# Hybrid attention/RG-LRU block: W loads of the first half of the tokens issued by PoolE instead of SyncE

## The chip, the cores and the metric

The kernel runs on one core of one Trainium2 chip. Five engines work beside each other, each through its own list of instructions in order: TensorE (PE in the profile; its weight loads are PEld), VectorE (DVE), ScalarE (ACT), PoolE or GpSimd (POOL) and SyncE (SP), which computes nothing here and issues most DMAs. An instruction waits for semaphores, and everything behind it on the same engine waits with it. The metric is the device time of one execution in microseconds (us), the median of several runs.

## The reference

One decoder block over 2048 tokens of width 1024. A combined projection gives q, k and v of three groups of heads, a gate of the attention, input and gate of a recurrent branch (RG-LRU), and two merge gates. Dilated banded attention and the recurrence follow; both are gated, projected, merged, projected again and normalized. The change concerns the first line of it:

```python
proj = x @ w_in[l] + b_in[l]          # (2048 x 1024) @ (1024 x 9216)
q, k, v, g_attn, u_lru, g_lru, gate_logits = jnp.split(proj, SPLIT_POINTS, axis=-1)
...
u = causal_depthwise_conv(u_lru, conv_w[l], conv_b[l])
h = rg_lru(u, lru_wr[l], lru_br[l], lru_wi[l], lru_bi[l], lru_lambda[l])
y_b = (h * jax.nn.silu(g_lru)) @ w_lru_proj[l]
```

All values are float32. The kernel splits each operand of a product into a high and a low part and forms three products of them.

## The kernel before

**Quads.** The projection takes the larger part of the time (about 0 to 1440 us of the span). It is cut into 72 quads: 36 for the first half of the tokens (`plan[s][0]` is 0, s from 0 to 35), the same 36 for the second (`plan[s][0]` is 1). A quad is two blocks of 128 output columns by two chunks of 512 tokens. Except for the first quad of all (s is 0), a quad is computed by Strassen's scheme with seven products instead of eight; their factors are blocks of W (A11, A12, A22) and sums of blocks (S1 to S4) on one side, and prepared blocks of x on the other. A product is 12 matmuls of 128x128 by 128x512 on PE (L632), four slices of depth with high and low parts. One product is one step of the program's clock `now["n"]`, and `base[s]` is the step at which quad s begins. A quad of the middle kind takes 7 steps.

**Where a block of W comes from.** `load_w` (L232) takes a slot of SBUF (one of 34, 128x512 float32, 256 KB, handed out in the order in which they became vacant) and loads a block from HBM. In the first half S1 and S3 are both loaded as A21, and then `added` (L242) adds A22 to the one and A11 to the other by an accumulating DMA, issued by POOL, that waits until the first load has landed. DVE adds S2 = S1 + A11 in `sums` and S4 = S2 + A12 in `add_w`. Then `prep_w` (L264) forms the high part on ACT (L269) and the low part on DVE (L227, a helper's line for all two-input operations). The low parts go to DRAM (L282), and the second half of the tokens loads them from there.

**The order.** It is written out ahead: events are put at steps, and each step emits its product and then its events, so each engine's list follows the steps. For the first half, with t0 four steps ahead of `base[s]`:

```python
for d, n in ((6, "S1"), (6, "S3"), (4, "A11"), (3, "A12"), (d22, "A22")):
    at(t0 - d, lambda s=s, n=n: load_w(s, n))
for n, x in (("S1", "A22"), ("S3", "A11")):
    at(max(t0 - 4, 2), lambda s=s, n=n, x=x: added(s, n, x))
...
at(max(t0 - 1, 4), lambda s=s: sums(s))
at(max(t0, 4), lambda s=s: add_w(s, "S4", "S2", "A12"))
```

For a quad of the middle kind `d22` is -1, so its A22 falls into the step of the S1 and S3 of the next quad, ahead of them.

**What else is in these lists.** SP issues, beside the loads of W: the swaps of halves for the rotary embedding (L307, four DMAs of 64 KB for each block of q or k), the stores of k, q, v (L330, L337, L347, L371), of gates and of the recurrence's input (L377, L396, L411, L419), and the low parts (L282). POOL has, in the first half, the accumulating DMAs, the loads of the small gate matrices (`fetch_gr`, L441, four of 16 KB each) and the product of the recurrence's result with its gate (L540, shown as L227 y<-y,h), which waits for the scan on DVE (L528). The gate matmuls of the recurrence (L493, output g) stand on PE between two halves of a product and read vh (ACT, L483) and vl (DVE).

After the projection come attention (to about 1650 us), the merge, and the output projection with the normalization; the change touches nothing there.

Of the kernel before, what the change touches and what calls it, by code (L numbers as in the profile page):

```python
# [15 lines left out]
P = 128  # L16
S = 2048
# [14 lines left out]
def hybrid_block_kernel(ctx: ExitStack, tc: tile.TileContext, a: dict, out: bass.AP):  # L32
    nc = tc.nc
    sp, act, dve, pool, pe = nc.sync, nc.scalar, nc.vector, nc.gpsimd, nc.tensor
# [98 lines left out]
    def take(name, dt=F32R):  # L133
        if not vacant:
            raise RuntimeError(f"no slot at {now['n']}: {[x[1].name if hasattr(x[1],'name') else x[1] for x in home.values()]} chains {len(chains)}")
        i = vacant[0]
        if name[0] == "y" and now["n"] >= base[NQ - 1]:
            i = next((x for x in LATE if x in vacant), i)
            if i in LATE:
                LATE.remove(i)  # L140
        vacant.remove(i)
        t = sl_p.tile([P, CH], dt, tag=f"s{i}", name=name)
        home[id(t)] = (i, t)
        return t
# [86 lines left out]

    def load_w(s, n):  # L232
        r = raw[s, n] = take(f"w{n}_{s}", F32)
        sp.dma_start(r.rearrange("p (k f) -> p k f", f=P), w_part(s, "A21" if n[0] == "S" else n))

    def w_part(s, n):

        f = plan[s][1][int(n[1]) - 1][0]
        k = 4 * (int(n[2]) - 1)
        return a["w_in"][f, :, k:k + 4, :]  # L240
# [318 lines left out]
    plan = []  # L559
# [142 lines left out]
    for s in range(1, NQ):  # L702
        t0 = base[s] - (3 if plan[s][0] else 4)
        if plan[s][2] is None:
            for d, n in ((4, "A21"), (4, "A11"), (3, "A22"), (3, "A12")):
                at(t0 - d, lambda s=s, n=n: load_w(s, n))
            for j in range(4):
                at(t0 + j, lambda s=s, j=j: prep_w(s, j))
            continue
        if plan[s][0]:  # L710
            for d, n in ((4, "A21"), (4, "A22"), (3, "A11"), (3, "A12")):
                at(t0 - d, lambda s=s, n=n: load_w(s, n))
        else:
            d22 = 3 if s == 1 else 4 - plan[s][2].index(4)
# [6 lines that stand above are left out]
        if plan[s][0]:  # L721
            at(t0, lambda s=s: sum3(s))
        for j in range(7):
            d = 3 if j == 6 and plan[s][2] is MID else 0
            if plan[s][0] and j % 2 == 0:
                at(t0 + j - 1 + d, lambda s=s, j=j: load_lo(s, j))
            at(t0 + j + d, lambda s=s, j=j: prep_w(s, j))
# [244 lines left out]
    n = len(where)  # L972
# [416 lines left out]
    for n in range(32):  # L1389
        c, f = divmod(n, 8)  # L1390
# [229 lines left out]
```

## Time and profile before

| | us |
|---|---|
| median of 3 runs | 2099.08 |
| lowest, highest | 2097.64, 2104.75 |
| the profiled execution, its own time | 2101.99 |
| its span, first to last instruction | 2100.3 |
| DVE busy in the span | 1676.0 |
| ACT busy in the span | 1093.1 |
| loads of W by SP, both halves | 253 (wA) and 70 (wS), 256 KB each |
| accumulating loads by POOL | 70, 256 KB each |

The profile is of one execution. In its rows a line such as L234 is the line of the kernel, the names behind the operation are out<-in with numbers left out (wA is a block A11, A12, A21 or A22, wS an S1 or S3), and what stands in brackets is the idle time of the engine just before and who ended it. In lists of waits the columns are the total in us, how many, and the longest. SPq is SP's queue. A DMA's time to landing runs from its issue to the last of its data.

### The profile page before, as it was taken

To read this page: it belongs to the slowest core of one execution; us is meant where nothing else is said; L and a number is where in the kernel's file an instruction comes from. 1 tells how busy PE (TensorE), PEld (TensorE's weight loads), DVE (VectorE), ACT (ScalarE), POOL (GpSimd) and SP (SyncE) were. 2 spreads that over 40 slices of the span, in tenths; PEclk is the share of its full clock that TensorE was granted. 3 is DMA by queue.
4 is the path that set the end of the run, shared out by engine and by line. 5 is a ranking of instruction groups with operands and counts; after the bars stand their busy time and mean duration, and the time that the engine had idled before them with its cause. 6 is when DMAs were issued, how large, how long until landed. Compare 5 with 4: busy or idle time off the path is not lost. (4 is left out here: it accounts for less than half of the span.)

```text
span 2100.3 us, 35032 instructions
## 1 busy us (share of the span) xinstructions
PE 2070.4 (99%) x11696; PEld 1706.2 (81%) x11696; DVE 1676.0 (80%) x3146; ACT 1093.1 (52%) x2293; POOL 474.9 (23%) x436
## 2 busy tenths in 40 slices
PE   8999999999999999999999999999999999999998
PEld 7888788788778888888888887888888888888887
DVE  8889789788788778888879887976999645576667
ACT  6347356346256566657666565666999411211100
POOL 1111111111111012231222232221424344331120
PEclk9999999999999999999999999999999999999999
DMA  9898988998988977878788879789896798864431
GB/s 273 270 251 250 263 261 248 281 247 264 235 284 233 319 229 203 243 206 232 235 271 255 283 225 260 230 244 352 317 345 206 228 305 273 299 223 157 156 106 71
DMA packets 369589, 516.26 MB, mean 246 GB/s; under 512 B 173056, under 2 KB 178176, under 8 KB 366080
## 3 DMA queue, kind: packets, MB, share of 16 engines
q1 hardware_dynamic: 349232, 480.63, 71.6%
q0 software_dynamic: 12256, 19.42, 5.6%
q10 hardware_dynamic: 7920, 13.97, 1.9%
q8 instruction: 93, 1.52, 0.3%
q14 instruction: 88, 0.72, 0.1%
HBM read 312.95 MB, written 186.25 MB: 238 GB/s over the span
## 5 line engine op out<-in xcount | busy, mean ns | idle before, releaser
L632 PE MATMUL q<-xT,hS 128*128 128x512 f32 x1680 | 519.2, 390 | 0.5 <-DVE y L227 0.5
L632 PE MATMUL q<-xT,l 128*128 128x512 f32 x1120 | 436.2, 389 | 0.0
L632 PE MATMUL q<-xB,hA 128*128 128x512 f32 x1248 | 389.9, 394 | 5.8 <-ACT xB L215 5.8
L632 PEld LDWEIGHTS q<-xT,hS 128*128 128x128 f32 x1680 | 314.2, 188 | 70.8 <-issue 6.1
L632 PE MATMUL q<-xB,l 128*128 128x512 f32 x904 | 354.0, 392 | 5.8 <-DMA l<-wl_scr 3.5
L632 PEld LDWEIGHTS q<-xB,hA 128*128 128x128 f32 x1248 | 235.7, 190 | 59.3 <-ACT xB L215 5.7
L632 PEld LDWEIGHTS q<-xT,l 128*128 128x128 f32 x1120 | 210.6, 188 | 43.9
L632 PEld LDWEIGHTS q<-xB,l 128*128 128x128 f32 x904 | 170.8, 189 | 44.2 <-DMA l<-wl_scr 5.1
L269 ACT ACTIVATE hA<-wA 128x512 fp32r<-128x512 f32 x218 | 135.0, 622 | 86.8 <-DMA wA<-in_w_in_dram 54.5
L632 PE MATMUL q<-xT,hA 128*128 128x512 f32 x560 | 174.1, 392 | 0.0
L245 POOL DMA_DIRECT2D wS<-in_w_in_dram x70 | 62.0, 978 | 493.8 <-DMA wS<-in_w_in_dram 201.5
L1051 ACT ACTIVATE p<-p,sta 128x256 f32<-128x256 f32 (+1 forms) x384 | 172.7, 468 | 1.1 <-DVE sta L1043 1.1
L632 PE MATMUL q<-xB,hS 128*128 128x512 f32 x560 | 172.6, 389 | 0.0
L269 ACT ACTIVATE hS<-S 128x512 fp32r<-128x512 f32 x175 | 107.8, 623 | 88.9 <-DVE S L227 42.6
L227 POOL TENSOR_TENSOR S<-S,wA 128x512 f32<-128x512 f32 x35 | 50.1, 1431 | 415.6 <-DVE S L227 214.6
L632 PEld LDWEIGHTS q<-xT,hA 128*128 128x128 f32 x560 | 105.1, 189 | 24.0 <-issue 2.5
L632 PEld LDWEIGHTS q<-xB,hS 128*128 128x128 f32 x560 | 105.1, 188 | 22.1 <-issue 0.4
L227 DVE TENSOR_TENSOR y<-y,cos 128x512 f32<-128x512 f32 x96 | 85.0, 888 | 43.3 <-DMA sw<-y 38.3
L1043 DVE CUSTOM_DVE_ANT_0 p<-s,mask 128x256 f32<-128x256 f32 (+1 forms) x384 | 116.4, 360 | 0.2 <-PE s L1036 0.2
L1479 PE MATMUL z<-wo,mh 128*128 128x512 f32 (+1 forms) x264 | 101.0, 383 | 0.0
L1480 PE MATMUL z<-wo,ml 128*128 128x512 f32 (+1 forms) x264 | 101.0, 383 | 0.0
L1478 PE MATMUL z<-wo,mh 128*128 128x512 f32 (+1 forms) x264 | 101.0, 383 | 0.0
(204 smaller groups left out, 4163.6 us busy)
## 6 DMA issues: line engine op xcount, KB each, us to landing
wA<-in_w_in_dram SPq DMA_DIRECT2D x253, 256.0 KB, 5.0
wl_scr<-l SPq DMA_DIRECT2D x105, 512.0 KB, 5.3
l<-wl_scr SPq DMA_DIRECT2D x105, 512.0 KB, 4.6
sw<-y SPq DMA_DIRECT2D x384, 64.0 KB, 3.1
wS<-in_w_in_dram SPq DMA_DIRECT2D x70, 256.0 KB, 4.6
wS<-in_w_in_dram POOLq DMA_DIRECT2D x70, 256.0 KB, 6.5
v_scr<-vs SPq DMA_DIRECT2D x192, 64.0 KB, 3.9
B<-k_scr SPq DMA_DIRECT2D x24, 512.0 KB, 7.5
```

Of the source, the lines that this page charges most:

```text
L227: eng.tensor_tensor(out=out, in0=in0, in1=in1, op=op)
L245: pool.dma_start(t, w_part(s, x), accum_op=ALU.add)
L269: act.activation(h, r, AF.Copy)
L632: pe.matmul(bank, w[:, ks], x[:, kk, xx], start=(first and i == 0 and not onto), stop=(last and i == 11), skip_group_check=onto)
L1043: dve.tensor_tensor_reduce(out=st["p", i, j][:, h, lo:256], in0=st["s", i, j // 2][h][:, j % 2, lo:256], in1=mask[:, lo:256], scale=1.0, s ...
L1051: act.activation(p, p, AF.Exp, scale=-1.0, bias=s[:, h:h + 1], accum_out=s[:, 2 + h:3 + h])
L1478: pe.matmul(z, mh[:, k], w[:, 0, hs], start=(k == 0), stop=False)
L1479: pe.matmul(z, mh[:, k], w[:, 1, hs], start=False, stop=False)
L1480: pe.matmul(z, ml[:, k], w[:, 0, hs], start=False, stop=(k == 7))
```

## The change

The engine that issues the DMA in `load_w` is chosen by the quad. The second half of the tokens and the first quad stay on SP; the other 35 quads of the first half go to POOL, five loads each. Slots, destinations, bytes and the steps at which the loads stand in the program are the same.

```diff
     def load_w(s, n):
         r = raw[s, n] = take(f"w{n}_{s}", F32)
-        sp.dma_start(r.rearrange("p (k f) -> p k f", f=P), w_part(s, "A21" if n[0] == "S" else n))
+        eng = sp if plan[s][0] or not s else pool
+        eng.dma_start(r.rearrange("p (k f) -> p k f", f=P), w_part(s, "A21" if n[0] == "S" else n))
```

## The prediction

> **What bounds the kernel now.** I read the busy shares first, then the two halves of the projection stage, then TensorE's waits in the first one, since that is where the moved loads lie.
>
> ```profile
> span 2100.3 us, 35032 instructions
> PE 2070.4 (99%) x11696; PEld 1706.2 (81%) x11696; DVE 1676.0 (80%) x3146; ACT 1093.1 (52%) x2293; POOL 474.9 (23%) x436
> ...
> 0.00:720.00 720.00, 704.37 (x3086) 573.87 (x3087) 609.09 (x976) 375.86 (x619) 98.10 (x127) 1.00 0.89 262
> ```
>
> The last row is the first half of the tokens: window, its length, busy us of PE, PEld, DVE, ACT, POOL, then granted clock, DMA share, GB/s. PE is busy 704.37 of 720 us, so the loads can win only from 15.6 us of idle time and from what the clock lost. POOL works 98 us of 720. The DMA engines are at 0.89, and the change moves no byte off them.
>
> TensorE's waits in that stretch, and the table of 20 us windows around the worst place:
>
> ```profile
> PE q L632 <- ACT xB L215: 5.8, 1, 5.8
> PE g L493 <- DVE vl L227: 5.1, 2, 2.6
> PE q L632 <- DVE l L227: 2.2, 2, 1.2
> PE g L493 <- ACT vh L483: 2.0, 1, 2.0
> PE q L632 <- DVE y L227: 0.5, 1, 0.5
> ...
> 580.00:600.00 20.00, 18.09 (x68) 14.31 (x69) 16.23 (x27) 17.11 (x26) 1.75 (x2) 0.83 0.97 327
> 600.00:620.00 20.00, 20.00 (x90) 16.57 (x89) 15.96 (x24) 6.21 (x11) 5.17 (x7) 1.00 0.78 233
> ```
>
> 5.8 us is the start, before the second quad, which the change leaves alone. 9.8 us remain: 7.1 in the gate matmuls (L493), 2.7 in L632. In 580 to 600 us the granted clock was 0.83 of full speed: 20 x 0.17 = 3.4 us lost on top. So **13.2 us** is all that the first half can give.
>
> Who caused these waits? The timelines of PE, DVE and ACT at the two stalls:
>
> ```profile
> 578.93 0.51 PE L493 MATMUL g<-vh,gw 64*128 64x512 f32 x2 [2.00 <-ACT vh L483]
> 581.91 0.79 PE L493 MATMUL g<-vl,gw 64*128 64x512 f32 x2 [2.48 <-DVE vl L227]
> ...
> 577.72 0.69 DVE L227 TENSOR_TENSOR S<-wS,wA 128x512 f32<-128x512 f32 x1 [2.60 <-DMA wA<-in_w_in_dram]
> 579.96 0.69 DVE L227 TENSOR_TENSOR S<-S,wA 128x512 f32<-128x512 f32 x1 [0.75 <-DMA wA<-in_w_in_dram]
> ...
> 577.73 0.63 ACT L269 ACTIVATE hA<-wA 128x512 fp32r<-128x512 f32 x1 [5.13 <-DMA wA<-in_w_in_dram]
> ...
> 261.86 0.50 PE L493 MATMUL g<-vl,gw 64*128 64x512 f32 x2 [2.64 <-DVE vl L227]
> ...
> 259.91 0.69 DVE L227 TENSOR_TENSOR S<-S,wA 128x512 f32<-128x512 f32 x1 [1.93 <-DMA wA<-in_w_in_dram]
> ```
>
> Both engines stood still for a block of W that had not landed: ACT 5.13 us, DVE 2.60 and 0.75, and, 318 us earlier, DVE 1.93. vh and vl, which the gate matmuls read, are queued behind these on ACT and DVE. So 2.00 + 2.48 + 2.64 = 7.1 us of PE idle, and the clock loss that follows the first pair at once, come from W loads that were late. Why late? SP's own timeline ahead of the second stall:
>
> ```profile
> 560.44 3.08 SPq L307 DMA_DIRECT2D sw<-y  x4
> ...
> 564.75 0.91 SPq L234 DMA_DIRECT2D wS<-in_w_in_dram  x2
> ...
> 566.91 3.02 SPq L377 DMA_DIRECT2D u_scr<-y  x1
> 569.98 1.61 SPq L371 DMA_DIRECT2D v_scr<-vs  x1
> 571.64 0.67 SPq L234 DMA_DIRECT2D wA<-in_w_in_dram  x1
> ...
> 573.31 1.26 SPq L234 DMA_DIRECT2D wA<-in_w_in_dram  x1
> ```
>
> Between the S loads and the A11 load, 6.9 us pass in which SP issues stores; one of them holds it 3.02 us, another 1.61. A11 was issued at 571.64 and ended the waits at 577.7, 6.1 us later. SP's order, not the transfer, made it late.
>
> **The change part by part.** For quads 1 to 35 five loads (S1, S3, A11, A12, A22) go from SP to POOL: 175 DMAs of 256 KB, the same bytes. The accumulating DMAs (L245) stay on POOL.
>
> ```profile
> L245 POOL DMA_DIRECT2D wS<-in_w_in_dram x70: 853/909/1244, 19.3 to 686.7; - x70
> ...
> DMA to landing us min/median/max: 3.8/6.5/9.1
> ...
> L441 POOL DMA_DIRECT2D gr<-in_wr_dram x32: 526/556/1220, 64.4 to 1325.0; - x32
> ...
> DMA to landing us min/median/max: 2.0/5.3/7.4
> ...
> DMA to landing us min/median/max: 2.7/4.6/9.5
> ```
>
> (Issues of the accumulating loads and their landing; of the 16 KB gate blocks and theirs; the last row is the landing of SP's W loads in 0 to 720.)
>
> A plain 256 KB load by POOL is not in this trace. Its issue lies between 0.56 (16 KB) and 0.91 us (same size, accumulating); I take 0.91, the row of the same size. From issue to landing it lies between SP's 4.6 and the accumulating 6.5; I take 6.5, again the row of POOL's own loads of this size. So each load costs 1.9 us more than on SP, once issued.
>
> POOL's load: per quad 7 DMAs x 0.91 = 6.4 us. A quad is 84 matmuls at 90 per 20 us, 18.7 us. Over 35 quads 175 x 0.91 = 159 us more on an engine that is busy 98 of 720: it fits, at no cost beside the order.
>
> Order on POOL: A22 of the old quad, S1, S3, A11, the two accumulates, A12. A12, and all of the next quad, now stand behind the accumulates' wait for S1 and S3. Suppose POOL began exactly at the step where the program places these loads. A22 starts at 0, S1 at 0.9, S3 at 1.8; S1 lands at 0.9 + 6.5 = 7.4, its accumulate starts then and lands at 13.9. The sum that needs it comes five steps of 12 matmuls later, 5 x 12 x 0.222 = 13.3 us: 0.6 us late (with 4.6 for the plain load, 1.3 early). The second accumulate starts at 8.3, A12 at 9.2 and lands at 15.7; it is needed at six steps, 16.0. What covers the 0.6 is that POOL need not wait for its step:
>
> ```profile
> SPq L234 <- DVE l L227: 16.3, 10, 3.7
> SPq L234 <- PE q L632: 4.7, 10, 0.8
> SPq L234 <- PE g L493: 4.1, 2, 2.9
> ...
> POOL wS L245 <- DMA wS<-in_w_in_dram: 201.5, 16, 23.9
> POOL y L227 <- DVE h L528: 79.7, 11, 13.7
> ```
>
> The first three rows are SP's largest waits for engines at the W loads, 25 us in 22 of 183 loads (113 and 70): mostly the slot was already free when SP came to it, so a queue with less in front issues earlier. POOL stood idle 201.5 us in 16 waits for S blocks issued by SP: it is ahead of SP, not behind. If the cover fails, DVE waits 0.6 us per quad, which its own lead over PE hides; only several us at once reached PE above.
>
> A bound on the other side: the W stalls of 577 to 582 us began with a load issued 6.9 us after the S loads. Even with 1.9 us more per transfer, 5 us are won there.
>
> SP loses 175 issues. By its median rows a W load holds it about half a microsecond, some 90 us of 720, so its other work comes earlier, above all the half swaps that DVE waits for:
>
> ```profile
> L234 SPq DMA_DIRECT2D wA<-in_w_in_dram x113: 327/518/3436, 0.8 to 717.3; - x113
> ...
> DVE y L227 <- DMA sw<-y: 35.9, 19, 3.7
> ...
> 555.41 0.69 DVE L227 TENSOR_TENSOR y<-y,cos 128x512 f32<-128x512 f32 x1 [1.41 <-DMA sw<-y]
> ...
> 558.62 0.50 PE L632 MATMUL q<-xB,l 128*128 128x512 f32 x1 [1.20 <-DVE l L227]
> ```
>
> The remaining 2.7 us of PE idle (L632) follow such DVE waits: 3 us before the 1.20 at 558.62 DVE had waited 1.41 for swapped halves. I count half of 2.7, 1.4 us; the ends are 0 and 2.7. It costs nothing where it fails.
>
> **Sum:** 7.1 + 3.4 + 1.4 = 11.9 us. The profiled execution took 2101.99 us (span 2100.3), so 2090.1. The median of the runs shown is 2099.08, 2.9 us less; theirs reach from 2097.64 to 2104.75, and I take it that they differ by just such stalls, so I don't subtract that again.
>
> [...] The rows of L245 show POOL issuing in 0.85 to 1.24 us while DVE was busy 609 of 720 us. [...]
>
> **The rivals.**
>
> *A. Loads in time, stalls gone:* the forecast, 2088.8 (all of 13.2) to 2093.
>
> *B. Hidden anyway.* The stalls are two accidents out of 35 quads. With DMA at 0.89, POOL's loads now compete with SP's stores instead of standing behind them; stores land later, slots come free later, and another quad gets the accident. For it: the share, and that DVE is busy 609 of 720, so little else gives way. Against it: no byte is added. If the larger stall (2.00 + 2.48 + 3.4 = 7.9) comes back once, 2090.1 + 7.9 = 2098.
>
> *C. POOL's order takes SP's place (slower).* POOL waits in order too: for h (L528) 79.7 us in 11 waits, at most 13.7, and for the slot of A11, ahead of the accumulates. Lead and need differ by 0.6 us the wrong way, so from the point where POOL begins a quad some 5 us behind its step (the length of the ACT wait that reached PE), PE stands, and the clock halves. Three such quads instead of the two now: 3 x 7.9 = 23.7, minus the 11.9 won, 2101.99 + 11.8 = 2114. POOL's idle time above speaks against it.
>
> *D. It does nothing.* If slots rather than SP set the issue of the loads, they move by nothing: 2099 to 2102. The waits at slots (25 us in 183 loads) speak against it.
>
> [...]
>
> **How the numbers follow.** A 0.55, B 0.26, C 0.12, D 0.04, E 0.03. A run of this kernel can be told from no change beyond some 0.3%, 6.3 us, that is below 2092.8 or above 2105.4. Most of A is faster, some of it within; B, D and E are within; C is slower. Faster 0.53, same 0.35, slower 0.12. Predicted 2090. The range leaves out C and a little of A's edge: low 2085 (all 13.2 with the runs' 2.9 below the profile), high 2102 (D).
>
> **What would show it.** Right: the W loads of a quad issued by POOL ahead of their old times, by 5 us or more at the old stalls; no wait of L493 over 1 us and no window of clock under 1.00 in the first half; ACT's and DVE's waits for wA near zero; fewer DVE waits for sw. Wrong: POOL waits for slots or for h with an accumulate behind, S sums waiting for wS, PE waits in other quads. If POOL's issue of a plain load is far over 0.91 us, or its landing over 6.5, the sum falls.

## The result and the profile after

| | before | after |
|---|---|---|
| median of 4 runs | 2098.55 us | 2121.55 us |
| lowest, highest | 2097.64, 2104.75 | 2118.53, 2122.74 |
| ratio, 95% interval | | 1.0101 (1.0079 to 1.0124) |
| the profiled execution | 2101.99 us | 2122.74 us |

The change made the kernel slower by 1%, 23 us. The prediction said 2090 with a range of 2085 to 2102, so the time lies outside it, and the kernel became slower where it was to become faster. In the rows of after, lines from 234 on have moved by one (L632 is L633, L307 is L308, L245 is L246, L493 is L494); the load of W is L235.

The head of the page of after, two rows of the table of windows (window, length, busy us of PE, PEld, DVE, ACT, POOL, granted clock, DMA share, GB/s), and TensorE's and VectorE's waits in the first half:

```profile
span 2121.0 us, 35087 instructions
...
PE 2077.7 (98%) x11696; PEld 1707.7 (81%) x11696; DVE 1678.5 (79%) x3146; ACT 1093.1 (52%) x2293; POOL 574.1 (27%) x611
```

```profile
260.00:280.00 20.00, 14.32 (x57) 10.92 (x56) 14.23 (x23) 9.62 (x17) 3.21 (x6) 0.83 0.93 246
580.00:600.00 20.00, 14.36 (x53) 11.35 (x52) 11.11 (x18) 8.65 (x17) 3.98 (x7) 0.83 0.98 257
```

```profile
PE q L633 <- DVE y L227: 14.6, 5, 5.7
PE q L633 <- ACT xB L215: 7.7, 4, 5.7
...
PE g L494 <- ACT ti L506: 0.9, 1, 0.9
...
PE g L494 <- DVE vl L227: 0.6, 2, 0.3
PE g L494 <- ACT vh L484: 0.3, 2, 0.2
...
DVE y L227 <- DMA sw<-y: 62.1, 21, 7.1
```

The stalls that the change was expected to remove are gone: before the gate matmuls, vl and vh now cost 0.9 us, against 7.1 before. The first three rows that follow are of before: DVE's waits for wA and wS, which are in no row of after, and ACT's for wA. The last row is what is left of ACT's in after: three waits in the first 20 us and one at 743.7 us, behind the first half.

```profile
DVE S L227 <- DMA wA<-in_w_in_dram: 6.2, 4, 2.6
...
DVE S L227 <- DMA wS<-in_w_in_dram: 3.8, 4, 1.7
...
ACT hA L269 <- DMA wA<-in_w_in_dram: 12.4, 6, 5.1
...
ACT hA L270 <- DMA wA<-in_w_in_dram: 5.7, 4, 2.2
```

What came instead is larger. TensorE's products waited 14.6 us for DVE's y (0.5 before), and DVE waited 62.1 us for swapped halves (35.9 before). Two of the new stalls hold most of it, each with a window at clock 0.83:

```profile
266.48 1.19 PE L633 MATMUL q<-xT,hS 128*128 128x512 f32 x2 [5.68 <-DVE y L227]
...
592.29 1.19 PE L633 MATMUL q<-xT,hS 128*128 128x512 f32 x2 [5.64 <-DVE y L227]
...
264.44 0.69 DVE L227 TENSOR_TENSOR y<-y,cos 128x512 f32<-128x512 f32 x1 [6.81 <-DMA sw<-y]
...
590.25 0.69 DVE L227 TENSOR_TENSOR y<-y,cos 128x512 f32<-128x512 f32 x1 [6.78 <-DMA sw<-y]
```

DVE stood 6.8 us at a swap, and the result that TensorE's next matmul waits for (y<-q, at 265.65 us) is queued behind it. Each of the two costs 5.6 to 5.7 us of idle, and some clock behind it: from 264 to 270 us the granted clock was 0.50 (as in before from 582 to 588 us), in part while TensorE stood still anyway. The 20 matmuls across the two stalls took 12.2 and 13.0 us, where 20 x 0.227 = 4.5 us is their pace elsewhere, so the two cost 7.7 + 8.5 = 16.2 us together.

**Where the time is lost.** If the start of the n-th matmul of after is set against that of before, after is 7.1 us late at the 42nd matmul (18.4 us in before) and still at the 504th, 20.0 late at the 3016th (704 us) and 19.7 late near the end. So all of it is lost in the first half, and a third of it in the first 20 us. The other 12.9 us are a difference: before had lost 13.2 us to its own stalls, which are gone, so the new ones behind the start cost some 26 us by estimate, twice as much.

**The start.** The timelines of POOL and SP of after, and SP's of before:

```profile
2.06 1.31 POOL L235 DMA_DIRECT2D wS<-in_w_in_dram  x2
3.36 1.60 POOL L235 DMA_DIRECT2D wA<-in_w_in_dram  x3
9.00 1.93 POOL L246 DMA_DIRECT2D wS<-in_w_in_dram  x2 [4.04 <-DMA wS<-in_w_in_dram]
...
10.32 10.01 SPq L221 DMA_DIRECT2D xcB<-in_xT_dram  x8
```

```profile
7.59 5.62 SPq L221 DMA_DIRECT2D xcB<-in_xT_dram  x8
```

POOL's list is empty at 2 us, so it issues the five W blocks of the second quad and both accumulates while SP still brings x for the first. The eight x loads began 2.7 us later and took 10.01 us to issue instead of 5.62, so the last was out 7.1 us later, the loss of the start. In both runs SP starts each of the eight 0.02 us after an earlier load has landed, and by 26 us it had waited 8.3 us for such landings ahead of x loads, against 3.1 in before. Before, the W blocks stood behind x in SP's list, from 13.59 us on.

**The swaps.** Around 255 us, in the timeline of after: SP's four DMAs of the fourth swap of a q/k pair, and POOL.

```profile
255.24 5.15 SPq L308 DMA_DIRECT2D sw<-y  x4
...
254.06 0.54 POOL L235 DMA_DIRECT2D wA<-in_w_in_dram  x1 [5.94 <-DVE rp L227]
254.59 1.86 POOL L246 DMA_DIRECT2D wS<-in_w_in_dram  x2
...
257.09 0.57 POOL L235 DMA_DIRECT2D wA<-in_w_in_dram  x1 [0.64 <-DMA k_scr<-rp]
```

The four issues of that swap in after, in the view of its line (least/median/most ns), and the swap, the W loads behind it and the accumulates in the timelines of SP and POOL of before:

```profile
L308 SPq DMA_DIRECT2D sw<-y x4: 527/1488/1517, 255.2 to 258.9; - x4
```

```profile
240.99 3.00 SPq L307 DMA_DIRECT2D sw<-y  x4
...
244.66 0.52 SPq L234 DMA_DIRECT2D wA<-in_w_in_dram  x1
245.22 0.91 SPq L234 DMA_DIRECT2D wS<-in_w_in_dram  x2
...
249.82 1.82 POOL L245 DMA_DIRECT2D wS<-in_w_in_dram  x2 [23.93 <-DMA wS<-in_w_in_dram]
```

In after, A11, both accumulates and A12 go out between 254.06 and 257.66, and the fourth swap between 255.24 and 260.39: 1 MB of W beside 256 KB of swap. In before the accumulates were issued 8.8 us after the swap, since S1 and S3, to which they add, stood behind it on SP. A11 waited on POOL for a slot that the third block's rp gives back, 5.94 us, so its moment is tied to the q/k chain. The landing is not all of the lateness. Set against TensorE's progress (how late the same matmul starts in after), SP issued the fourth swap 3.6 us later than in before at the first of the two stalls and 0.8 at the second; from first issue to last landing it took 9.1 and 8.9 us, against 4.4 and 4.5. The landing of all swaps of the first half, before and then after (least, median, most):

```profile
DMA to landing us min/median/max: 1.9/3.0/7.6
```

```profile
DMA to landing us min/median/max: 1.9/4.1/9.9
```

### The profile page after: what moved, and what is told of

Read it like the earlier page. It is cut to its first block, busy times and chain, and to the rows that moved or that the text cites. A ratio compares the mean times of both kernels' runs of the same rounds, so it can differ in the third digit from the quotient of the medians.

```text
span 2121.0 us, 35087 instructions
## 1 busy us (share of the span) xinstructions
PE 2077.7 (98%) x11696; PEld 1707.7 (81%) x11696; DVE 1678.5 (79%) x3146; ACT 1093.1 (52%) x2293; POOL 574.1 (27%) x611
## 5 line engine op out<-in xcount | busy, mean ns | idle before, releaser
L633 PE MATMUL q<-xT,hS 128*128 128x512 f32 x1680 | 522.7, 393 | 14.6 <-DVE y L227 14.6
L633 PE MATMUL q<-xT,l 128*128 128x512 f32 x1120 | 437.2, 390 | 0.0
L633 PE MATMUL q<-xB,hA 128*128 128x512 f32 x1248 | 391.5, 395 | 8.8 <-ACT xB L215 7.7
L633 PEld LDWEIGHTS q<-xT,hS 128*128 128x128 f32 x1680 | 316.2, 189 | 86.8 <-issue 21.7
L633 PE MATMUL q<-xB,l 128*128 128x512 f32 x904 | 354.5, 392 | 6.3 <-DMA l<-wl_scr 3.4
L633 PEld LDWEIGHTS q<-xB,hA 128*128 128x128 f32 x1248 | 235.4, 189 | 65.6 <-ACT xB L215 9.6
L633 PEld LDWEIGHTS q<-xT,l 128*128 128x128 f32 x1120 | 211.3, 189 | 44.3
L633 PEld LDWEIGHTS q<-xB,l 128*128 128x128 f32 x904 | 170.9, 189 | 45.2 <-DVE l L227 5.4
L633 PE MATMUL q<-xT,hA 128*128 128x512 f32 x560 | 173.1, 390 | 0.0
L633 PE MATMUL q<-xB,hS 128*128 128x512 f32 x560 | 172.5, 389 | 0.0
L235 POOL DMA_DIRECT2D wA<-in_w_in_dram x105 | 67.5, 643 | 337.4 <-DVE l L227 123.5
L633 PEld LDWEIGHTS q<-xT,hA 128*128 128x128 f32 x560 | 104.7, 188 | 23.6 <-issue 2.2
L633 PEld LDWEIGHTS q<-xB,hS 128*128 128x128 f32 x560 | 105.0, 188 | 22.1 <-issue 0.4
```

What stands on the lines that cost most here:

```text
L235: eng.dma_start(r.rearrange("p (k f) -> p k f", f=P), w_part(s, "A21" if n[0] == "S" else n))
L633: pe.matmul(bank, w[:, ks], x[:, kk, xx], start=(first and i == 0 and not onto), stop=(last and i == 11), skip_group_check=onto)
```

## The experiments

Theory 1: POOL runs ahead of SP, and its accumulates and A loads move the same bytes at the very time of the fourth swap, which DVE needs at once; the swap lands late. Theory 2: it is the start alone, or the mere use of POOL's queue, or the A loads. All of the edits below stand in `load_w` unless another place is shown. The table gives all runs; each ratio is to the runs of before taken beside it, whose medians were 2098.55 to 2099.87 us. "Fourth swap" is the time from the first issue to the last landing of the four DMAs, least to most, in the profiled execution of each, for six of the twelve q/k pairs: those whose fourth swap landed latest in after (tiles sw12_1, sw21_1, sw22_1, sw16_1, sw23_1, sw18_1). The other six took 3.8 to 4.7 us in before and 5.0 to 7.9 in after.

| run | what goes out by POOL | median us | ratio to before, 95% interval | DVE waits for sw, us | fourth swap, us |
|---|---|---|---|---|---|
| before | accumulates | 2098.55 | | 35.9 | 3.8 to 5.8 |
| after | all loads, quads 1 to 35 | 2121.55 | 1.0101 (1.0079 to 1.0124) | 62.1 | 8.3 to 10.8 |
| e1_from_quad3 | all loads, quads 3 to 35 | 2115.00 | 1.0068 (1.0053 to 1.0083) | 66.0 | 8.1 to 10.6 |
| e2_a_on_pool | only A11, A12, A22, from quad 3 | 2099.33 | 1.0001 (0.9990 to 1.0011) | 43.8 | 5.0 to 7.1 |
| e3_s_on_pool | only S1, S3, from quad 3 | 2107.04 | 1.0033 (1.0020 to 1.0047) | 58.8 | 4.9 to 8.9 |
| e4_traffic | as before, and useless copies at the swap | 2118.08 | 1.0086 (1.0071 to 1.0101) | 61.6 | 5.3 to 8.8 |
| e5_after_swap | as e1, accumulates held behind the swap | 2099.91 | 1.0004 (0.9995 to 1.0012) | 42.1 | 3.8 to 5.2 |
| e6_start_only | all loads of quads 1 and 2 alone | 2105.89 | 1.0041 (1.0029 to 1.0054) | 40.6 | 3.8 to 6.0 |
| e7_wait_only | as before, with e5's hold | 2098.31 | 1.0001 (0.9992 to 1.0010) | 35.5 | 3.8 to 5.8 |
| e8_a_after_swap | as e2, with e5's hold | 2101.51 | 1.0014 (1.0005 to 1.0023) | 39.8 | 4.4 to 5.7 |
| e9_a12_early | as e5, A12 two steps earlier | 2097.37 | 0.9989 (0.9980 to 0.9998) | 42.4 | 4.5 to 6.4 |
| e10_a12_early_sp | as e7, A12 two steps earlier on SP | 2096.98 | 0.9990 (0.9979 to 1.0000) | 37.3 | 3.8 to 5.8 |

### The start taken out

```diff
-        eng = sp if plan[s][0] or not s else pool
+        eng = sp if plan[s][0] or s < 3 else pool
```

> As the changed kernel, but POOL's loads begin with quad 3; those of quads 1 and 2 stay on SP. Theory 1 (contention): at the start POOL's loads of quads 1 and 2, issued from 2 us on, share the DMA engines with SP's loads of x; in the changed kernel PE is 7.1 us behind by its 42nd matmul. Expected: these 7 us come back whole, 2121.5 falls to about 2114.5, and the other losses stay. Theory 2 (POOL's own order is what costs, the start is something else): 2121 as before.

The start came back: the 42nd matmul begins 0.5 us earlier than in before. 13.5 us of the profiled execution stayed lost, with the same signature. The waits, POOL and SP of this run:

```profile
PE q L633 <- DVE y L227: 17.1, 5, 6.2
```

```profile
247.40 0.54 POOL L235 DMA_DIRECT2D wA<-in_w_in_dram  x1 [4.98 <-DVE rp L227]
247.92 1.84 POOL L246 DMA_DIRECT2D wS<-in_w_in_dram  x2
...
249.34 5.07 SPq L308 DMA_DIRECT2D sw<-y  x4
```

So the start costs about 6.5 us of 23, and what comes behind it, by theory 1 the meeting at the swap, the other 16.

### The loads apart

```diff
-        eng = sp if plan[s][0] or s < 3 else pool
+        eng = sp if plan[s][0] or s < 3 or n[0] == "S" else pool
```

> From quad 3 on POOL loads only A11, A12 and A22; S1 and S3 stay on SP, so the accumulating DMAs wait for SP's loads again and go out about 9 us after the fourth swap of a quad pair instead of in it. Theory 1 (the accumulates, each over twice a plain load in DMA time, collide with the fourth swap): that swap lands in about 5 us after its issue instead of 9, DVE's longest wait for sw falls from 7 to under 4 us, time 2092 to 2102. Theory 2 (any W load on POOL's queue delays the swaps, or the order on POOL does): 2108 to 2115, as with POOL from quad 3.

With A11, A12 and A22 on POOL and S1 and S3 on SP, nothing is lost, though DVE's longest wait for a swap, 5.6 us, is over the expected 4. The accumulates wait for the S loads, which stand behind the swap on SP again. In DMA time an accumulate is nearly twice a plain load, not over twice, by an estimate from POOL's queue in the first 720 us: it took 15.9% of the 16 engines' time in before, nearly all of it for the 70 accumulates, and 36.5% in after with the 175 loads beside them, so some 26 us of one engine each against some 14. The waits of this run:

```profile
PE g L494 <- DVE vl L227: 3.9, 2, 2.9
PE q L633 <- DVE y L227: 3.6, 2, 2.1
```

The other half, S1 and S3 on POOL alone (`or n[0] == "A"` in place of `"S"`):

> The other part alone: from quad 3 on POOL loads S1 and S3, SP keeps A11, A12 and A22. The accumulates are early. Theory 1 (accumulates against the fourth swap): the stalls near 260 and 590 us stay, 2108 to 2116. Theory 2 (all POOL loads share the blame alike): half of the loss, 2103 to 2108.

It lost 7 us, half of e1_from_quad3. That lies in the range of theory 2, but equal shares are contradicted by e2_a_on_pool, which lost nothing. The largest row was the new one again; the accumulates and the fourth swap ahead of the first stall follow it:

```profile
PE q L633 <- DVE y L227: 10.9, 3, 5.5
...
239.65 0.88 POOL L246 DMA_DIRECT2D wS<-in_w_in_dram  x1 [2.35 <-DMA wS<-in_w_in_dram]
241.00 0.88 POOL L246 DMA_DIRECT2D wS<-in_w_in_dram  x1 [0.47 <-DMA v_scr<-vs]
...
245.95 3.42 SPq L308 DMA_DIRECT2D sw<-y  x4
```

The two halves do not add: 0 and 7 apart, about 14 to 16 together. Early accumulates alone do half of the harm, A loads alone none, both together all of it. But here the accumulates do not go out beside the fourth swap: they are issued 6.3 and 5.0 us ahead of it. The swap landed in 6.0 us (4.4 in before), and set against TensorE's progress SP issued it 5.0 us later than in before; at the second stall, near 578 us, it was 6.2 us (4.5 in before) and 3.4 us. So the half that this run shows comes through a late issue more than through a late landing, and what delayed the issue is not shown.

### The same traffic without the change

In the kernel before, at the fourth swap, a POOL copy that holds the place and four copies of 256 KB from HBM to HBM that nobody reads:

```diff
+        if c == 1 and not isq:
+            pool.tensor_copy(tick, flat(rw)[:, 0:1])
+            for b in range(4):
+                pool.dma_start(junk[b], a["w_in"][f, :, 4 * (b % 2):4 * (b % 2) + 4, :].rearrange("p k f -> p (k f)"))
```

> The kernel before, all W loads on SP in their old order, with nothing changed in what is computed; at the fourth swap of each of the 12 pairs of q and k POOL issues four more copies of 256 KB from HBM to HBM that nobody needs. Theory 1 (DMA time shared with POOL's queue is what delays the swap): the fourth swap lands in 7 to 10 us instead of 4.5, DVE waits for it, and the time is 2106 to 2125. Theory 2 (it is an order of loads and slots, not DMA time): the swap lands within 1 us of before, 2098 to 2103.

All W loads lie on SP in their old order here, and 1 MB copied by POOL (issued from 244.94 to 247.06 us, the swap from 247.14) costs 18 us with the same two rows on top:

```profile
PE q L638 <- DVE y L227: 9.5, 4, 3.7
...
DVE y L227 <- DMA sw<-y: 61.6, 23, 5.9
```

This adds bytes, which the change does not, and not all of its cost need come through the swap, since DVE's waits for wS rose too, from 3.8 to 8.6 us. So it shows that traffic at that moment is enough, not that it is what happened. The next one asks that.

### The accumulates held behind the swap

As e1_from_quad3, with one small POOL instruction in `qk_chain`. It reads a swapped tile that DVE has multiplied, so everything behind it in POOL's list waits until the swap has landed:

```diff
             tt(dve, flat(sw), flat(sw), sin, ALU.mult)
+            if c == 1 and not isq:
+                pool.tensor_copy(tick, flat(sw)[:, 0:1])
```

> From quad 3 on all five loads by POOL, as in e1_from_quad3 (2115), and one POOL copy of 128x1 that reads the fourth swapped tile of a q/k pair after DVE has multiplied it. In POOL's order it stands ahead of A11 and the accumulates of the quads whose swap was late (sw12_1, sw21_1 and their like), so these can't start before the swap has landed; bytes, queue and packets stay. Theory 1 (accumulates and A loads that run at the same moment as the fourth swap make it land late): the fourth swaps land in 7 us at most (7.3 to 10.6 in e1_from_quad3), TensorE's waits for DVE y fall from 17.1 to under 5 us, and the time to 2092 to 2103. Theory 2 (it is enough that POOL's queue takes part, with its larger packets, whenever that is): 2110 to 2118, the swaps late as before.

The 16 us are gone. The W loads, their bytes and their queues (80 packets for a load of 256 KB on POOL's, 144 on SP's, by the queues' totals in before and after) are those of e1_from_quad3; only the moment has moved, so the moment is the cause. How much of it acts through the landing of the fourth swap and how much through its later issue is not separated. SP and POOL at the same place:

```profile
243.09 2.88 SPq L310 DMA_DIRECT2D sw<-y  x4
...
248.92 0.18 POOL L317 COPY tick<-sw 128x1 f32<-128x1 f32 x1 [11.95 <-DVE sw L227]
249.56 0.54 POOL L235 DMA_DIRECT2D wA<-in_w_in_dram  x1 [0.46 <-issue]
250.09 1.84 POOL L246 DMA_DIRECT2D wS<-in_w_in_dram  x2
```

POOL waited 11.95 us, the swap was out in 2.88 us instead of 5.07, and the six fourth swaps landed in 3.8 to 5.2 us. The other six took up to 8.5 us, and DVE's waits for swaps stayed at 42.1 us, above the 35.9 of before. TensorE's waits show what came back:

```profile
PE g L498 <- DVE vl L227: 5.0, 3, 2.4
...
PE q L637 <- DVE y L227: 1.7, 2, 1.1
```

TensorE's waits for DVE's y fell from 17.1 to 1.7 us, and the old stall at the gate matmuls returned with 5.0. The same hold in the kernel before changes nothing, so it neither costs nor wins by itself:

> The kernel before with the POOL copy of e5_after_swap alone (all W loads on SP). Control: theory 1 says that the accumulates of the kernel before already go out after the swap, so the copy changes nothing: 2097 to 2101. If the copy or its wait costs by itself: above 2105, and e5_after_swap has to be read against this.

And with the A loads alone on POOL it was 0.14% slower than before, half a microsecond above its expectation:

> A11, A12, A22 on POOL from quad 3 on as in e2_a_on_pool (2099.3, fourth swaps 4.7 to 7.1), with the POOL copy of e5_after_swap. Theory 1: little is left to win, 2094 to 2101; the fourth swaps land in 6.5 us at most. If the wait makes the sums late: above 2105, with DVE waiting for wS.

### The start alone

```diff
+        eng = sp if plan[s][0] or s not in (1, 2) else pool
```

> Only quads 1 and 2 on POOL, all others on SP as before. If the start costs 7 us by itself and nothing gives it back: 2104.5 to 2107. If the 7 us were only taken over from stalls that come later anyway: 2098 to 2102.

Ten loads out of 175 cost 0.41% (0.29 to 0.54), 6.7 us between the medians of that comparison (2099.24 for before). The matmuls are 7.5 us late from the 168th to the 1000th, and 4.9 near the end.

### A version that might beat both

In e5_after_swap two stalls of the old kind were left, where a sum had waited for A12. So A12 was put ahead of A11 and the accumulates, once on POOL and once on SP:

```diff
-            for d, n in ((6, "S1"), (6, "S3"), (4, "A11"), (3, "A12"), (d22, "A22")):
+            for d, n in ((6, "S1"), (6, "S3"), (4, "A11"), (5 if s >= 3 else 3, "A12"), (d22, "A22")):
```

> e5_after_swap (2099.9: loads on POOL from quad 3 on, accumulates held behind the swap) with A12 loaded two steps earlier in the program, so that it stands on POOL ahead of A11 and the accumulates instead of behind them. In e5_after_swap two stalls of the old kind are left: 2.36 us at 262 and 2.10 at 580 us before the gate matmuls, behind a sum on DVE that had waited for A12 (1.2 us at 260). If A12's place behind the accumulates makes them: S<-wA waits of DVE under 1.5 us in all, the two stalls under 1 us, and the time 2092 to 2096, faster than both kernels. If the earlier A12 takes its slot or its DMA time from something else, as the change did: 2099 to 2108, with DVE's waits for sw up again.

> The same earlier A12 with all W loads on SP (e7_wait_only, 2098.3, and A12 two steps earlier). If the early place alone does it and POOL as issuer adds nothing: within 2 us of e9_a12_early. If SP's stores still stand ahead of A11 and hold the sums: 2097 to 2101 while e9_a12_early is faster.

Both are some 2 us under before, less than can be told from no change by the bound of 0.3%, and equal to each other; the expectation of 2092 to 2096 was missed. In e9_a12_early no wait of DVE for W is left in the first half, as expected, and the granted clock is 1.00 in all of its windows (0.998 over the whole execution). TensorE stood idle nevertheless:

```profile
PE q L637 <- DVE y L227: 3.6, 2, 2.0
PE q L637 <- DVE l L227: 3.0, 2, 1.6
PE g L498 <- DVE vl L227: 2.1, 2, 1.1
PE g L498 <- ACT ti L510: 0.8, 1, 0.8
```

That is 3.6 + 3.0 + 2.1 + 0.8 = 9.5 us, against 9.8 in before. The waits for W went, and the waits for swaps rose from 35.9 to 42.4 us. Of the issuers tried, none gained.

## Why the prediction was wrong

**"5.8 us is the start, before the second quad, which the change leaves alone."** This failed. The wait itself stayed, 5.7 us in after, and the change leaves the first quad's loads on SP, but not what lies beside them: the rest of that quad came later. With an empty list POOL starts the next quads' blocks at 2.06 us, while x is still being loaded; the start grew by 7.1 us, and e6_start_only reproduces it alone. The row that would have told it was in the timeline of POOL of before, where it waited 17.16 us for an S block that SP issued only at 13.59:

```profile
19.28 2.00 POOL L245 DMA_DIRECT2D wS<-in_w_in_dram  x2 [17.16 <-DMA wS<-in_w_in_dram]
```

**The old stalls, 7.1 + 3.4.** The reading was right as far as it went: loads that stood behind SP's stores made ACT and DVE wait. By POOL the A11 of the two old stalls goes out 8 and 12 us earlier against TensorE's progress, and those waits vanish. ("SP's order, not the transfer" is too strong: A11 landed 6.0 us after its issue, where the median row says 4.6.) It failed as a gain. e9_a12_early has no wait of DVE for W left, and none of ACT between 8 and 719 us, and is as fast as before within 0.3%. Taking away what ended a wait last gave the next one its turn: DVE's waits for swaps rose. That W blocks landing earlier are what makes the swaps land later there, with the DMA engines at 0.89 in before, is a reading of the rows and was not tested by itself.

**"SP loses 175 issues ... so its other work comes earlier, above all the half swaps ... It costs nothing where it fails."** This is the step that failed most: a term that was held to be a gain or nothing was the largest cost. I counted SP's issuing time and gave the swaps 1.4 us, between 0 and 2.7. They became the bound: DVE's waits for them rose from 35.9 to 62.1 us, and the stalls that followed made 16 of the 23 us. The swaps left SP at the same place in its order, but SP's order had kept the accumulates away from them, since those had to wait for S loads that stood behind the swap. I read POOL's 201.5 us of waiting as room to run ahead in and so as cover. It was the spacing, and the change removed it.

**The sizes.** POOL's issue and landing were taken too high, on the safe side:

```profile
L235 POOL DMA_DIRECT2D wA<-in_w_in_dram x105: 538/566/1317, 3.4 to 715.3; - x105
...
L235 POOL DMA_DIRECT2D wS<-in_w_in_dram x70: 538/538/755, 2.1 to 702.3; - x70
...
DMA to landing us min/median/max: 2.7/5.0/8.9
```

0.54 to 0.57 us each, not 0.91, and 5.0 to landing, not 6.5. POOL's busy time rose by 574.1 - 474.9 = 99.2 us in 175 loads, 0.57 each. The estimate that POOL has room held. Of the signs of being right that the prediction named, the earlier loads, the short waits at the gate matmuls (0.9 us at most) and the waits for W near zero came; the full clock and the fewer waits for swaps did not.

**The rivals.** B had the right kind of reason, transfers that compete with what SP issues. It named the stores and the slots as victims, where the swaps are what DVE waits for within microseconds, and priced it at one stall of the old size, 2098; with the collision out of the way, e5_after_swap and e9_a12_early measure 2099.9 and 2097.4, near its 2098. C had the sign, and its 2114 is near e1_from_quad3 by chance, for its reason is not what happened: no sum waited for wS or wA in after, so POOL was too early, not late. D is refuted: loads moved by microseconds. For the 0.03 of E no run shows a cause: in after POOL issued each moved load in 0.54 to 0.57 us at the median, under the 0.91 of the forecast.

With POOL's transfers beside them six of SP's swaps landed in 8.3 to 10.8 us instead of 3.8 to 5.8. And relieving SP of 175 issues did not only save its time here: it also dissolved an order that was worth 16 us.

**What stays open.** That the moment at which POOL's loads go out makes the difference is shown by e5_after_swap. By what path is shown only in part: the fourth swaps land late, and SP also issues them late, most of all in e3_s_on_pool. Whether the harm depends on the kind of DMA was not separated either: early accumulates did more than early A loads, but the two also went out at different moments. W loads on a third engine's queue were not tried.

## What to carry to other kernels

A single queue that issues everything is also a schedule: before moving part of it to an idle engine, list which of the transfers left behind are needed within microseconds, and look what the moved ones will run beside once nothing holds them back. Long idle waits of the new issuer (201.5 us here) are not free room; they say how far its work will jump ahead, at the start of the kernel above all. Where loads by a second engine are wanted, tie them to the step at which they may start (here one tiny instruction gave 15 us back), and with DMA engines as busy as here (0.89 in the first half of before) be ready to trade one late transfer for another rather than to win: in e9_a12_early DVE's 10.0 us of waits for W went and its waits for swaps rose from 35.9 to 42.4 us.

## What was not expected of the hardware

SP's own issue of a swap was slower in after: the four at 255 us took 5.15 us, 1.49 each at the median, where the four took 3.00 us in before and 2.88 with the accumulates held behind the swap (e5_after_swap). An issue is therefore not a fixed cost, and what stands behind it in the list waits. That POOL's transfers are the reason is not shown: in e4_traffic, beside 1 MB of POOL's copies, the four at 247 us took 3.17 us. And a plain load costs POOL 0.54 to 0.57 us to issue where an accumulating load of the same 256 KB costs it 0.91 (median of 70 in before).
